# A decoder layer on one core: the down projection with moving weights and a seven-product block form

## The chip, the cores and the metric

The kernel runs on one core of a Trainium2 chip. The metric is device time in microseconds (us). The core's engines are TensorE (PE; PEld is its weight load), VectorE (DVE), ScalarE (ACT), GpSimd (POOL) and SyncE (SP, which only issues DMAs here; ACT issues some too). Each engine works through its own instructions in their written order.

## The reference

```python
o = concat(diff_attention(...), multiscale_pool(...)) ; x = x + o @ w_o
x = x + cross_attention(rmsnorm(x), rmsnorm(mem))              # ends with @ wo_x
hf = rmsnorm(x) * norm_ffn
x = x + (silu(hf @ w_gate) * (hf @ w_up)) @ w_down             # 2048 -> 5632 -> 2048
out = rmsnorm(x) * norm_final                                  # over the 2048 features
```

There are 256 tokens and 2048 features; all is float32. The change concerns the last two lines.

## The kernel before, in words

Every float32 product is made of float32r parts: a value is split into hi (a cast on ACT, L111) and lo = value - hi (a subtraction on DVE, L112), and a product is hi*hi + hi*lo + lo*hi, summed in PSUM. With a gain the split is L114 on ACT and L115 on DVE.

The residual stream x_sb and the activations lie transposed, features on partitions. In a projection to features (`gemm_feat`) the weight tile is stationary and 256 tokens move: for each k-tile of 128, one matmul of 512 columns (hi weights, both parts of the activations, L145) and one of 256 (lo weights, hi activations, L146). Weights come from HBM in loads of 1 MiB (L127, SP's queue, three buffers `raw`), and are split in halves `whi` and `wlo`, three buffers each, so that splits can run ahead of the matmuls. Where the result is wanted with tokens on partitions (`gemm_tok`, L191 to L193), the weights move in 512 columns, three matmuls a block.

The stages in order: input projection, attention and pooling, w_o (from 205 us), cross-attention (w_qx, w_kx, w_vx, w_ox), gate and up (w_gu, 672 us to 1177 us) and down (w_dn, to 1421 us). In the w_o stage the 256 memory tokens are also loaded (L505), split (L114, L115) and squared (L252 on ACT; L254 and L257 add on POOL), while x is updated (L262, L264), split again and its squares are summed (L268, L270 on POOL). Gate and up leave their tiles to DVE and ACT: L206 copies one part out of PSUM, L207 joins, L615 and L618 scale, L616 is Silu, L619 multiplies, and a split stores the activations.

Down is one more `gemm_feat`, with 16 feature tiles of 44 k-tiles; the last tile uses three matmuls of 256 columns (L199 to L201) to shorten its end. As each tile ends, x is updated, squared (L268) and multiplied by the final gain (L628); at the first tile a Sqrt is run early (L631). After the last tile: ones-matmuls add the squares over partitions (L236), Sqrt (L226), reciprocal (L227), a transpose spreads 1/rms along the free dimension (L246), and seven multiplications (L639) each feed an output DMA (L640).

A scheduler orders each engine's instructions; the order in the text is not the order that runs. `between` holds small pieces of work that it spreads among the weights.

Of the kernel before, what the change touches and what calls it, by code (L numbers as in the profile page):

```python
# [12 lines left out]
"""  # L13
# [18 lines left out]
P = 128  # L32
D = 2048
S = 256
# [8 lines left out]
FT = DFF // P  # L43
NB = D // 512

# columns of the array of per-partition parameters
# [5 lines left out]
def layer_kernel(ctx: ExitStack, tc: tile.TileContext, a: dict, out: bass.AP):  # L52
    nc = tc.nc
    const = ctx.enter_context(tc.tile_pool(name="const", bufs=1))
    act = ctx.enter_context(tc.tile_pool(name="act", bufs=15))
    wts = ctx.enter_context(tc.tile_pool(name="wts", bufs=3))
    tmp = ctx.enter_context(tc.tile_pool(name="tmp", bufs=5))
    row = ctx.enter_context(tc.tile_pool(name="row", bufs=4))
    st = ctx.enter_context(tc.tile_pool(name="st", bufs=4))
# [13 lines left out]
    def chunk():  # L73
        """4 k-tiles of split, transposed activations: [128, k-tile, hi / lo, 256 tokens]."""
        return slot().rearrange("p (j s t) -> p j s t", j=4, s=2)
# [45 lines left out]
    def weights(src, n=2048, piece=2048, load=None):  # L121
        """Up to 1 MiB of weights, as halves of (hi, lo)."""
# [50 lines left out]
    def gemm_tok(xT, src, load=None):  # L173
        """512 features of both token tiles: two of [128 tokens, 512]."""
# [22 lines left out]
    def mm3(ps, l, r, start=True, stop=True):  # L197
        """ps (+)= l.T @ r of split operands."""
# [4 lines left out]
    def joined(ps):  # L203
        """The sum of a feature tile's parts."""
# [5 lines left out]
    def features(xT, src, f0, n=4):  # L210
        """n feature tiles, split: a chunk."""
# [6 lines left out]
    def values(ps, r):  # L218
        """[128 tokens, hi / lo, token tile, 512 features] times the tokens' r."""
# [10 lines left out]
    def rms(*squares, rc=None):  # L230
        """1/rms of the tokens, with tokens on partitions: [128, 2]."""
# [10 lines left out]
    def along(rc):  # L242
        """The same along the free dimension, on every partition (in PSUM)."""
# [5 lines left out]
    def add_squares(tot, c, src):  # L249
        """The sum of squares of chunks of [128, 4 x 256], in the end as one tile."""  # L250
# [8 lines left out]
    def residual(f, ps, tot, g=None, into=None, one=False):  # L259
        """x += ps for a feature tile; its scaled split, and the squares added up."""  # L260
# [23 lines left out]
    # the tensor engine's clock rises while the first loads are under way  # L284
# [5 lines left out]
    hT = []  # L290

    def load_x(k):
        """k-tile k of x: the first eight one by one, then four at a time."""
# [5 lines left out]
        if j == 0:  # L299
            hT.append(chunk())  # L300
# [22 lines left out]
    # pooling: for every window the matrix of (window sum - count * token), and 1 / count  # L323
# [81 lines left out]
    def diff_head(h, qk):  # L405
# [29 lines left out]
        wps = misc().rearrange("p (k q) -> p k q", k=2)  # [128 keys, key tile, queries]  # L435
# [18 lines left out]
    def norm_heads(half, o):  # L454
        """Two heads' outputs: norm over 256 features, gain, transposed."""
# [69 lines left out]
    tot1 = t_row()  # L525
    hx = []
    for f, ps in gemm_feats(lambda: oT, a["w_o"]):
        if f % 4 == 0:
            hx.append(chunk())
        residual(f, ps, tot1, col(C_XAT + f), hx[-1])  # L530

# [16 lines left out]
    def cross_head(h, kx):  # L548
# [19 lines left out]
        pps = misc().rearrange("p (k q) -> p k q", k=2)  # [128 memory tokens, tile, queries]  # L568
# [28 lines left out]

    tot2 = t_row()
    hf = []
    for f, ps in gemm_feats(lambda: xo, a["w_ox"]):  # L600
        if f % 4 == 0:
            hf.append(chunk())
        residual(f, ps, tot2, col(C_FFN + f), hf[-1])

# [1 line left out]
    aT = []  # L606
    for f in range(FT):
        if f % 4 == 0:
            aT.append(chunk())
        ps = gemm_feat(hf, a["w_gu"][2 * f])  # L610
        if f == 0:
            rb_f = t_row()
            nc.vector.tensor_copy(out=rb_f, in_=along(rms(tot2)))
        g = joined(ps)
        nc.vector.tensor_tensor(out=g, in0=g, in1=rb_f, op=ALU.mult)  # L615
        nc.scalar.activation(out=g, in_=g, func=AF.Silu)  # L616
        y = joined(gemm_feat(hf, a["w_gu"][2 * f + 1]))
        nc.vector.tensor_tensor(out=y, in0=y, in1=rb_f, op=ALU.mult)  # L618
        nc.vector.tensor_tensor(out=g, in0=g, in1=y, op=ALU.mult)  # L619
        split(aT[-1][:, f % 4, 0], aT[-1][:, f % 4, 1], g)  # L620

# [1 line left out]
    tot3 = t_row()  # L623
    rc_y = const.tile([P, 2], F32, name="rc_y")
    for f in range(KT):
        last = f == KT - 1
        sq = residual(f, gemm_feat(aT, a["w_dn"][f], FT, one=last), tot3, one=last)
        nc.scalar.activation(out=x_sb[:, f], in_=x_sb[:, f], func=AF.Copy, scale=col(C_FIN + f))  # L628
        if f == 0:
            # the table of Sqrt is there before it is waited for  # L630
            nc.scalar.activation(out=rc_y, in_=tot3[:, :2], func=AF.Sqrt)  # L631
# [76 lines left out]
```

## Time and profile before

| | us |
|---|---|
| median of 3 runs | 1432.77 (1432.4 to 1434.15) |
| span of the profiled execution | 1431.9 |
| PE busy | 1417.8 (99%) |
| DVE busy | 897.3 (63%) |
| ACT busy | 715.0 (50%) |
| down stage, PE busy from 1176 to 1421 | 245.0 of 245 |
| from the last down matmul (1420.5) to the end | 11.4 |

The span is the time from the first to the last instruction of one profiled execution; the median is 0.87 us above it. A matmul's own duration is longer than its step: consecutive ones overlap, so the step is read from start to start. Idle time of DVE or ACT matters only where PE waits for it.

### The profile page before, as it was taken

How to read it: one execution, taken by the hardware profiler on the slowest of the kernel's cores; microseconds unless marked ns; L12 is line 12 of the kernel's file. 1: busy time of each engine (PE TensorE's matmuls, PEld its weight loads, DVE VectorE, ACT ScalarE, POOL GpSimd, SP SyncE). 2: the span in 40 equal slices, each digit the busy share in tenths (PEclk: the TensorE clock that was granted, in tenths of full speed). 3: DMA queues.
4: the chain of work that ended last, by engine and by line, in shares of the span. 5: the costliest groups of instructions: out<-in, count | busy, mean ns of one | idle time of the engine just before them, and what ended most of it. 6: DMA issues, size and time to landing. Idle time of an engine off the chain costs nothing.

```text
span 1431.9 us, 20153 instructions
## 1 busy us (share of the span) xinstructions
PE 1417.8 (99%) x8050; PEld 1240.2 (87%) x8050; DVE 897.3 (63%) x1229; ACT 715.0 (50%) x1064; POOL 104.6 (7%) x118
## 2 busy tenths in 40 slices
PE   8999999999999999999999999999999999999997
PEld 6888888888888888888888888888888888888886
DVE  6666867975556555577666666666666664454443
ACT  6555755664454444455544444444444444444442
POOL 3700001410000000011000000000000000010010
PEclk9999999999999999999999999999999999999999
DMA  7544436555544445365455555555555555555552
GB/s 267 205 169 171 173 121 246 182 204 184 199 176 164 163 167 180 122 219 192 177 195 187 189 193 182 201 181 202 178 200 182 195 181 191 184 191 194 182 194 107
DMA packets 41565, 264.54 MB, mean 185 GB/s; under 512 B 4736, under 2 KB 6016, under 8 KB 13312
## 3 DMA queue, kind: packets, MB, share of 16 engines
q1 hardware_dynamic: 41184, 262.69, 52.0%
q8 instruction: 63, 1.03, 0.3%
q10 hardware_dynamic: 288, 0.57, 0.1%
q14 instruction: 30, 0.25, 0.0%
HBM read 261.14 MB, written 2.10 MB: 184 GB/s over the span
## 4 chain that ended last, share of the span: by engine, by line
PE 97%; DVE 1%; DMA 1%; ACT 0%; SPq 0%; issue 0%; DVEq 0%; ACTq 0%
PE acc L145 53%; PE acc L146 28%; PE acc L192 4%; PE acc L193 4%; PE acc L191 4%; PE ms L200 1%; PE ms L201 1%; PE ms L199 1%; DMA raw<-in_w_vu 1%; DVE wlo L112 1%; PE acc L201 0%; PE acc L200 0%; PE acc L199 0%; DVE act L115 0%; PE ms L380 0%; DVE x_sb L639 0%
## 5 line engine op out<-in xcount | busy, mean ns | idle before, releaser
L145 PE MATMUL acc<-act,whi 128*128 128x512 f32 x3348 | 1169.6, 393 | 0.0
L146 PE MATMUL acc<-act,wlo 128*128 128x256 f32 x3348 | 938.4, 280 | 0.4 <-DVE wlo L112 0.3
L112 DVE TENSOR_TENSOR wlo<-raw,whi 128x1024 fp32r<-128x1024 f32 (+1 forms) x500 | 608.1, 1217 | 456.5 <-ACT whi L111 453.8
L111 ACT CAST whi<-raw 128x1024 fp32r<-128x1024 f32 (+1 forms) x500 | 515.1, 1030 | 583.0 <-PE acc L145 336.4
L145 PEld LDWEIGHTS acc<-act,whi 128*128 128x128 f32 x3348 | 627.0, 187 | 141.0
L146 PEld LDWEIGHTS acc<-act,wlo 128*128 128x128 f32 x3348 | 632.7, 189 | 1.5 <-DVE wlo L112 1.4
L270 POOL TENSOR_TENSOR row<-row,t 128x256 f32<-128x256 f32 x44 | 46.3, 1053 | 1151.4 <-ACT t L268 1151.4
L191 PE MATMUL acc<-whi,act 128*128 128x512 f32 x256 | 101.0, 396 | 1.8 <-ACT whi L111 1.8
L192 PE MATMUL acc<-wlo,act 128*128 128x512 f32 x256 | 100.7, 393 | 1.1 <-DVE wlo L112 1.0
L193 PE MATMUL acc<-whi,act 128*128 128x512 f32 x256 | 100.4, 392 | 0.0
L111 ACT CAST act<-t 128x256 fp32r<-128x256 f32 x92 | 37.1, 404 | 57.9 <-DVE t L207 57.4
L192 PEld LDWEIGHTS acc<-wlo,act 128*128 128x128 f32 x256 | 48.5, 190 | 12.4 <-DVE wlo L112 2.7
L191 PEld LDWEIGHTS acc<-whi,act 128*128 128x128 f32 x256 | 48.3, 189 | 12.3 <-ACT whi L111 2.7
L207 DVE TENSOR_TENSOR t<-acc,t 128x256 f32<-128x256 f32 x136 | 56.8, 418 | 1.3 <-ACT t L206 1.2
L193 PEld LDWEIGHTS acc<-whi,act 128*128 128x128 f32 x256 | 48.4, 189 | 10.2
L206 ACT COPY t<-acc 128x256 f32<-128x256 f32 x136 | 49.8, 366 | 0.4 <-PE acc L146 0.4
L112 DVE TENSOR_TENSOR act<-t,act 128x256 fp32r<-128x256 f32 x92 | 38.7, 421 | 17.6 <-ACT act L111 17.2
L115 DVE SCALAR_TENSOR_TENSOR act<-x_sb,sm,act 128x256 fp32r<-128x256 f32 x48 | 38.9, 821 | 0.4 <-ACT act L114 0.4
L262 DVE TENSOR_TENSOR x_sb<-acc,x_sb 128x256 f32<-128x256 f32 x48 | 20.1, 419 | 17.4 <-PE acc L146 11.4
L114 ACT ACTIVATE act<-x_sb,sm 128x256 fp32r<-128x256 f32 x48 | 23.8, 508 | 8.2 <-DVE x_sb L264 6.1
L268 ACT ACTIVATE t<-x_sb 128x256 f32<-128x256 f32 x45 | 18.3, 406 | 9.0 <-DVE x_sb L262 7.2
L264 DVE TENSOR_TENSOR x_sb<-acc,x_sb 128x256 f32<-128x256 f32 x47 | 19.8, 421 | 1.0
(144 smaller groups left out, 577.0 us busy)
## 6 DMA issues: line engine op xcount, KB each, us to landing
raw<-in_w_gu SPq DMA_DIRECT2D x88, 1024.0 KB, 4.8
raw<-in_w_dn SPq DMA_DIRECT2D x32, 1024.0 KB, 4.9
raw<-in_w_qk SPq DMA_DIRECT2D x16, 1024.0 KB, 4.8
raw<-in_w_qx SPq DMA_DIRECT2D x16, 1024.0 KB, 4.8
raw<-in_w_kx SPq DMA_DIRECT2D x16, 1024.0 KB, 4.8
raw<-in_w_vx SPq DMA_DIRECT2D x16, 1024.0 KB, 4.8
raw<-in_w_vu SPq DMA_DIRECT2D x12, 1024.0 KB, 4.8
raw<-in_w_o SPq DMA_DIRECT2D x12, 1024.0 KB, 4.8
```

Of the source, the lines that this page charges most:

```text
L111: nc.scalar.copy(out=hi, in_=src)
L112: nc.vector.tensor_tensor(out=lo, in0=src, in1=hi.bitcast(F32), op=ALU.subtract)
L114: nc.scalar.activation(out=hi, in_=src, func=AF.Copy, scale=g)
L115: nc.vector.scalar_tensor_tensor(out=lo, in0=src, scalar=g, in1=hi.bitcast(F32), op0=ALU.mult, op1=ALU.subtract)
L145: nc.tensor.matmul(ps, whi[:, w], x, start=(k == 0), stop=False)
L146: nc.tensor.matmul(ps[:, :S], wlo[:, w], x[:, 0], start=False, stop=(k == nk - 1))
L191: nc.tensor.matmul(ps[t], xh, whi[:, w], start=(k == 0), stop=False)
L192: nc.tensor.matmul(ps[t], xh, wlo[:, w], start=False, stop=False)
L193: nc.tensor.matmul(ps[t], xl, whi[:, w], start=False, stop=(k == KT - 1))
L206: nc.scalar.copy(out=y, in_=ps[:, S:])
L207: nc.vector.tensor_tensor(out=y, in0=ps[:, :S], in1=y, op=ALU.add)
L270: nc.gpsimd.tensor_tensor(out=tot, in0=tot, in1=sq, op=ALU.add)
```

## The change

The down projection is turned round. Activations are stationary (128 tokens of a k-tile), weights move in 512 columns, and the result has tokens on partitions. It runs in two halves of 1024 output columns (b) times 22 pairs of k-tiles (p). A pair is a 2 x 2 block product (2 token tiles x 2 k-tiles, times 2 k-tiles x 2 column blocks). For 15 pairs it is made of eight block products; for the seven pairs 0, 2, ..., 12 (FAST) of seven products of sums (a Strassen-Winograd form), the sums of the activations made in the gate and up stage (four DVE operations of 128 x 128 a pair), those of the weights in `prep` (L725, L727, L728), and the seven results recombined in `sums`. Each block product is three matmuls of 512 columns (`mm3`, L211 to L213).

The residual x must therefore be in rows: `to_rows` makes 32 PE transposes of 128 x 128 with 8 ACT copies, written to DRAM during w_ox and gate/up and read back later (L765). The final norm sums squares along the free dimension (ACT Square with its accumulator, L735), multiplies by a gain row (L736), and scales by 1/rms per partition (L843, L845); four output DMAs of 512 KB take the place of seven. Pools are rearranged: `act` has 11 buffers instead of 15, `hid` has 4 for the streamed activations, and the down stage's buffers (2 `raw`, 1 `sum`) lie on the memory of those that the gate and up stage has left.

```diff
+FAST = tuple(range(0, 14, 2))
-    act = ctx.enter_context(tc.tile_pool(name="act", bufs=15))
+    hid = up.enter_context(tc.tile_pool(name="hid", bufs=4, side="right"))
+    act = before.enter_context(tc.tile_pool(name="act", bufs=11))
...
+    def to_rows(q):
+        yield
+        for t in range(2):
+            yield
+            tp = misc()
+            for i in range(4):
+                nc.tensor.transpose(out=tp[:, i * P:(i + 1) * P], in_=x_sb[:, 4 * q + i, t * P:(t + 1) * P], identity=ident)
+            xr = t2()
+            nc.scalar.copy(out=xr, in_=tp)
+            nc.scalar.dma_start(out=x_dram[q // 2, :, t, (q % 2) * 512:(q % 2 + 1) * 512], in_=xr)
...
-    for f in range(KT):
-        last = f == KT - 1
-        sq = residual(f, gemm_feat(aT, a["w_dn"][f], FT, one=last), tot3, one=last)
...
+    def prep(b, p):
+        raw = dn_r.tile([P, 4, 512], F32, tag="raw", name=name("raw"))
+        nc.sync.dma_start(out=raw.rearrange("p s n -> p (s n)"), in_=a["w_dn"][b, p])
...
+        if p not in FAST:
+            yield halves(raw[:, 0:2], 2, dn_u, "u")
+            yield halves(raw[:, 2:4], 2, dn_u, "u")
+            return
+        s = dn_r.tile([P, 4, 512], F32, tag="sum", bufs=1, name=name("sum"))
+        nc.vector.tensor_tensor(out=s[:, 0:2], in0=b12[:, None].to_broadcast([P, 2, 512]), in1=raw[:, 0:2], op=ALU.subtract)
+        yield halves(raw[:, 0:3], 3, dn_a, "a")
+        nc.vector.tensor_tensor(out=s[:, 2], in0=b22, in1=s[:, 0], op=ALU.subtract)
+        nc.vector.tensor_tensor(out=s[:, 3], in0=b21, in1=s[:, 2], op=ALU.subtract)
+        yield halves(s[:, 0:2], 2, dn_u, "u")
+        yield halves(s[:, 2:4], 2, dn_u, "u")
...
+        for i, ps in enumerate(C):
+            y = ys[b][i // 2][:, (i % 2) * 512:(i % 2 + 1) * 512]
+            nc.vector.tensor_tensor(out=y, in0=ps, in1=y, op=ALU.add)
+            if b:
+                finished(b, i // 2, i % 2)
...
+            nc.vector.memset(ss, 1.0)
+            between.append(late())
+    for t in range(2):
+        r = const.tile([P, 1], F32, name=f"r{t}")
+        nc.vector.tensor_reduce(out=r, in_=ss[:, t], axis=AX.X, op=ALU.add)
+        rsqrt(r, r, D)
...
+            (nc.scalar if b == 0 else nc.sync).dma_start(out=out[:, t, b * 1024:(b + 1) * 1024], in_=y)
```

The first place is SP's queue in the w_o stage, before; the numbers behind the names are buffers, `raw` takes weights, `act` the memory tokens.

```order
L127 DMA raw_2294<-in_w_o 128x1024
L127 DMA raw_2324<-in_w_o 128x2048
L127 DMA raw_2375<-in_w_o 128x2048
L127 DMA raw_2425<-in_w_o 128x2048
L127 DMA raw_2479<-in_w_o 128x2048
L127 DMA raw_2532<-in_w_o 128x2048
L505 DMA act_2428<-in_memT 128x1024 x2
```

The same place in the changed kernel.

```order
L139 DMA raw_2302<-in_w_o 128x1024
L517 DMA act_2436<-in_memT 128x1024
L139 DMA raw_2332<-in_w_o 128x2048
L517 DMA act_2436<-in_memT 128x1024
L139 DMA raw_2383<-in_w_o 128x2048
L517 DMA act_2781<-in_memT 128x1024
L139 DMA raw_2433<-in_w_o 128x2048
L517 DMA act_2781<-in_memT 128x1024
```

The four loads of the memory tokens stand five and more weight loads earlier; their 16 splits on ACT (L126) and DVE (L127) and the POOL additions move with them.

The second place is ACT's queue in the changed kernel where gate and up end and down begins: `acc_10709` is the last up tile, `aC` a stored activation, `ah` and `uh` the hi parts of down's first weights.

```order
L654 COPY t1f_10752<-acc_10709 128x256
L123 CAST aC_10560<-t1f_10660 128x256
L765 DMA y_11120<-x_dram 128x1024 x2
L123 CAST ah_10787<-raw_10783 128x1536
L123 CAST uh_10802<-sum_10785 128x1024
L123 CAST uh_10812<-sum_10785 128x1024
```

DVE's queue at the same place, in the changed kernel.

```order
L655 TENSOR_TENSOR t1f_10752<-acc_10709,t1f_10752 128x256
L688 TENSOR_TENSOR t1f_10752<-t1f_10752,rb_f 128x256
L690 TENSOR_TENSOR t1f_10660<-t1f_10704,t1f_10752 128x256
L124 TENSOR_TENSOR aC_10560<-t1f_10660,aC_10560 128x256
L725 TENSOR_TENSOR sum_10785<-raw_10783 128x1024
L727 TENSOR_TENSOR sum_10785<-raw_10783,sum_10785 128x512
L728 TENSOR_TENSOR sum_10785<-raw_10783,sum_10785 128x512
L124 TENSOR_TENSOR al_10788<-raw_10783,ah_10787 128x1536
L124 TENSOR_TENSOR ul_10803<-sum_10785,uh_10802 128x1024
```

All work on down's first weights stands behind the finishing of the last up tile, on both engines; before, the first split of down (L111, L112) stood ahead of it.

The third place is the end: DVE in the changed kernel, `acc` the four results of the second half, `g` the gain row.

```order
L822 TENSOR_TENSOR y_11931<-acc_11587,y_11931 128x512
L822 TENSOR_TENSOR y_11932<-acc_11588,y_11932 128x512
L736 TENSOR_TENSOR y_11931<-y_11931,g_11973 128x512 x2
L736 TENSOR_TENSOR y_11932<-y_11932,g_11973 128x512
L822 TENSOR_TENSOR y_11932<-acc_11589,y_11932 128x512
L838 TENSOR_REDUCE r_12426<-ss 128x1
```

ACT there, in the changed kernel.

```order
L735 ACTIVATE d_12423,ss<-y_11932 128x512
L238 ACT_TABLE_LOAD
L238 ACTIVATE r_12426<-r_12426,eps 128x1
L238 ACTIVATE r_12434<-r_12434,eps 128x1
L843 ACTIVATE y_11120<-y_11120,r_12426 128x1024
```

Three gain multiplications stand ahead of the last addition, and a table load between the last Square and Sqrt. The early Sqrt that the text has in `late` (L830), with its table load, stands at ACT's very start, ahead of the first split of x.

## Rows read from the trace of the kernel before

**Rows 1.** The page: span; chain of waits, share of the span by engine

```profile
span 1431.9 us, 20153 instructions
...
PE 97%; DVE 1%; DMA 1%; ACT 0%; SPq 0%; issue 0%; DVEq 0%; ACTq 0%
```

**Rows 2.** Windows: length, busy us of PE, PEld, DVE, ACT, POOL; clock; DMA share; GB/s

```profile
672.00:1176.00 504.00, 504.00 (x2910) 444.14 (x2909) 327.94 (x455) 246.28 (x366) 3.80 (x4) 1.00 0.53 189
1176.00:1421.00 245.00, 245.00 (x1458) 217.94 (x1456) 116.98 (x129) 106.57 (x128) 18.95 (x14) 1.00 0.53 177
```

**Rows 3.** Timeline of PE: start, duration, line; pairs, last tile, moving weights

```profile
1178.74 0.39 PE L145 MATMUL acc<-act,whi 128*128 128x512 f32 x1
...
1180.47 0.39 PE L145 MATMUL acc<-act,whi 128*128 128x512 f32 x1
...
1413.75 0.28 PE L199 MATMUL acc<-act,whi 128*128 128x256 f32 x1
...
1420.47 0.28 PE L201 MATMUL acc<-act,wlo 128*128 128x256 f32 x1
...
59.66 0.39 PE L191 MATMUL acc<-whi,act 128*128 128x512 f32 x1
...
62.38 0.39 PE L191 MATMUL acc<-whi,act 128*128 128x512 f32 x1
```

**Rows 4.** Timeline of ACT where down begins

```profile
1177.32 0.37 ACT L206 COPY t<-acc 128x256 f32<-128x256 f32 x1
```

**Rows 5.** Timeline of DVE where down begins

```profile
1177.45 1.23 DVE L112 TENSOR_TENSOR wlo<-raw,whi 128x1024 fp32r<-128x1024 f32 x1 [1.81 <-ACT whi L111]
1178.59 0.42 DVE L207 TENSOR_TENSOR t<-acc,t 128x256 f32<-128x256 f32 x1
```

**Rows 6.** The page: cast of weights; busy us, mean ns

```profile
L111 ACT CAST whi<-raw 128x1024 fp32r<-128x1024 f32 (+1 forms) x500 | 515.1, 1030 | 583.0 <-PE acc L145 336.4
```

**Rows 7.** Groups of DVE in the down stage: count, busy us, mean ns

```profile
L112 DVE TENSOR_TENSOR wlo<-raw,whi 128x1024 fp32r<-128x1024 f32 x78 | 95.4, 1223 | 104.9 <-ACT whi L111 104.9
L112 DVE TENSOR_TENSOR wlo<-raw,whi 128x512 fp32r<-128x512 f32 x16 | 11.1, 692 | 17.4 <-ACT whi L111 17.4
```

**Rows 8.** Timeline of PE in the start, idle before in brackets

```profile
20.06 0.73 PE L191 MATMUL acc<-whi,act 128*128 128x512 f32 x2 [1.14 <-ACT whi L111]
...
22.93 0.63 PE L192 MATMUL acc<-wlo,act 128*128 128x512 f32 x1
23.36 0.63 PE L193 MATMUL acc<-whi,act 128*128 128x512 f32 x1
```

**Rows 9.** Windows in the w_o stage

```profile
228.00:256.00 28.00, 28.00 (x162) 24.29 (x161) 24.59 (x35) 17.80 (x29) 5.04 (x6) 1.00 0.69 250
266.00:286.00 20.00, 19.57 (x108) 16.29 (x107) 19.48 (x20) 12.98 (x20) 14.51 (x8) 1.00 0.52 199
```

**Rows 10.** Timeline of DVE in the w_o stage: two memory splits; a weight split

```profile
267.45 0.89 DVE L115 SCALAR_TENSOR_TENSOR act<-act,sm,act 128x256 fp32r<-128x256 f32 x2
...
279.40 2.65 DVE L112 TENSOR_TENSOR wlo<-raw,whi 128x1024 fp32r<-128x1024 f32 x1
```

**Rows 11.** Timeline of POOL in the w_o stage

```profile
278.45 2.52 POOL L254 TENSOR_TENSOR act<-act 128x1024 f32<-128x1024 f32 x1 [1.17 <-ACT act L252]
```

**Rows 12.** Timeline of PE: eight transposes, from first start to last end

```profile
159.17 1.03 PE L469 MATMUL ms<-ident,act 128*128 128x128 f32 x8
```

**Rows 13.** Timeline of SP's queue: the first six of seven output DMAs

```profile
1424.15 3.62 SPq L640 DMA_DIRECT2D out<-x_sb  x6
```

**Rows 14.** Timeline of ACT: a table load and what follows

```profile
45.63 1.28 ACT L226 ACT_TABLE_LOAD   x1
46.93 0.26 ACT L226 ACTIVATE rc<-ms,eps 128x1 f32<-128x1 f32 x1
```

**Rows 15.** DMA issues: KB, median us to landing; down's weights

```profile
raw<-in_w_dn SPq DMA_DIRECT2D x32, 1024.0 KB, 4.9
```

**Rows 16.** DMA issues from 235 to 300

```profile
act<-in_memT SPq DMA_DIRECT2D x4, 512.0 KB, 6.4
```

More of the change, by code (lines that the diff above doesn't have):

```diff
@@ L601, in layer_kernel @@
         if f % 4 == 0:
-            hf.append(chunk())
+            hf.append(chunk(True))
         residual(f, ps, tot2, col(C_FFN + f), hf[-1])
[L606 to L620, printed above, removed]
@@ L635, in layer_kernel @@
[L635 to L641 removed]
+        if f % 4 == 3:
+            between.append(to_rows(f // 4))
+    ps_g = gemm_feat(hf, a["w_gu"][0])
+    rb_f = const.tile([P, S], F32, name="rb_f")
@@ new lines, in layer_kernel, with t1f, joined_f @@
+    nc.vector.tensor_copy(out=rb_f, in_=along(rms(tot2)))
+    ps_u = gemm_feat(hf, a["w_gu"][1])
+    finish()
+    before.close()
+    aTp = ctx.enter_context(tc.tile_pool(name="aT", bufs=1, reuse_waits="tile"))
+    t1p = up.enter_context(tc.tile_pool(name="t1p", bufs=6, reuse_waits="tile"))
+    A11, A12, A22, S1, S2, S3, S4, A21 = range(8)
+    sides = []
+    def t1f():
+        return t1p.tile([P, S], F32, tag="t1f", name=name("t1f"))
+    def joined_f(ps):
+        y = t1f()
+        nc.scalar.copy(out=y, in_=ps[:, S:])
+        nc.vector.tensor_tensor(out=y, in0=ps[:, :S], in1=y, op=ALU.add)
+        return y
@@ new lines, in finished, with sums @@
+    def finished(b, t, h):
+        y = ys[b][t][:, h * 512:(h + 1) * 512]
+        nc.scalar.activation(out=d512(), in_=y, func=AF.Square, accum_out=ss[:, t, 2 * b + h:2 * b + h + 1])
+        nc.vector.tensor_tensor(out=y, in0=y, in1=gs[b][:, h * 512:(h + 1) * 512], op=ALU.mult)
+    def sums(b, M):
+        y = [[ys[b][t][:, h * 512:(h + 1) * 512] for h in range(2)] for t in range(2)]
+        add = lambda o, x, z: nc.vector.tensor_tensor(out=o, in0=x, in1=z, op=ALU.add)
+        p1, u2, u3 = d512(), d512(), d512()
+        nc.scalar.copy(out=p1, in_=M[0])
+        yield
+        add(u2, M[3], p1)
+        yield
+        add(u3, M[4], u2)
+        add(y[0][0], y[0][0], p1)
+        yield
+        add(y[1][0], y[1][0], u3)
+        add(u2, M[2], u2)
+        yield
+        add(y[0][1], y[0][1], u2)
+        add(u3, M[2], u3)
+        yield
+        add(y[1][1], y[1][1], u3)
@@ new lines, in load_rows, with load_gains @@
+    def load_rows(b):
+        if b == 0:
+            t = dec.tile([P, 2, 1024], F32, tag="y", bufs=1, name="y0")
+            ys[b] = [t[:, 0], t[:, 1]]
+        else:
+            ys[b] = [aTp.tile([P, 1024], F32, tag="C", bufs=FP - len(FAST), name=name("y1")) for _ in range(2)]
+        for t in range(2):
+            nc.scalar.dma_start(out=ys[b][t], in_=x_dram[b, :, t])
+        yield
+    def load_gains():
+        for b in range(2):
+            gs[b] = aTp.tile([P, 1024], F32, tag="C", bufs=FP - len(FAST), name=name("g"))
+            nc.scalar.dma_start(out=gs[b], in_=a["gain"][:, b * 1024:(b + 1) * 1024].to_broadcast([P, 1024]))
+        yield
@@ new lines, in layer_kernel, with into, late @@
+    pending = []
+    for b in range(2):
+        M = {}
+        C = [acc() for _ in range(4)]
+        def into(ps, w, n, p, last=False):
+            mm3(ps, sides[p][n], w, id(ps) not in M, last or (p in FAST[-1:] and any(ps is q for q in shared)))
+            M[id(ps)] = True
+        shared = [misc() for _ in range(4)] if FAST else []
+        for p in range(FP):
+            parts = prep(b, p)
+            if p in FAST:
+                b11, b22, b21 = next(parts)
+                tick()
+                into(shared[0], b11, A11, p)
+                into(C[1], b22, S4, p)
+                into(C[0], b21, A12, p)
+                s1, s3 = next(parts)
+                into(shared[1], s1, S1, p)
+                into(shared[3], s3, S3, p)
+                tick()
+                s2, s4 = next(parts)
+                into(shared[2], s2, S2, p)
+                into(C[2], s4, A22, p)
+            else:
+                b11, b22 = next(parts)
+                tick()
+                into(C[0], b11, A11, p)
+                into(C[2], b11, A21, p)
+                into(C[1], b22, A12, p)
+                into(C[3], b22, A22, p)
+                b21, b12 = next(parts)
+                tick()
+                last = p == FP - 1
+                into(C[0], b21, A12, p, last)
+                into(C[1], b12, A11, p, last)
+                into(C[2], b21, A22, p, last)
+                into(C[3], b12, A21, p, last)
+            if p == 8 or (not FAST and p == 0):
+                between.append(load_rows(b))
+            if b == 1 and p == 9:
+                between.append(load_gains())
+            if p == 14 and FAST:
+                between.append(sums(b, [shared[0], None, shared[1], shared[2], shared[3]]))
+        finish()
+        for i, ps in enumerate(C):
[3 more added lines that the diff above has]
+                finished(b, i // 2, i % 2)
+        if b == 0:
+            def late():
+                for _ in range(26):
+                    yield
+                nc.scalar.activation(out=ss[:, :, 0], in_=ss[:, :, 0], func=AF.Sqrt)
+                for i in range(4):
+                    finished(0, i // 2, i % 2)
+                    yield
+            nc.vector.memset(ss, 1.0)
+            between.append(late())
```

109 lines of the change are left out of this document (81 added, 28 removed).

## Prediction

> **What bounds the kernel now.** I read the chain of waits first: 97% of it is PE [rows 1]. The windows by stage say the same of the two stages that matter most here: gate and up, and down, have PE busy in every microsecond, while DVE is busy 117 of 245 us in down [rows 2]. So a matmul taken away from down is time saved, one for one, and anything that makes PE wait, or gives it other work, is time added. The timeline of PE then gives the steps. Five pairs of a 512- and a 256-column matmul take 1180.47 - 1178.74 = 1.73 us, 0.346 each; the last tile takes 6.72 us for 56 steps, 0.120 each; where weights move, twelve 512-column matmuls take 2.72 us, 0.2267 each [rows 3]. Last I read the three places at which the order changes: the w_o stage, the seam between gate/up and down, and the end.
>
> **The matmuls.** Before: 15 x 44 pairs x 0.346 = 228.4, and 132 x 0.120 = 15.8, together 244.2 us, which agrees with the window of 245. After: 2 halves x (15 pairs x 8 + 7 pairs x 7) products x 3 = 1014 matmuls x 0.2267 = 229.9 us. This is **-14.3 us**. The moving-weight rows are float32r matmuls of the same shape, each with a new stationary tile, so I carry nothing for the form.
>
> The Trainium skill, "TensorE: Matmul & The Clock Gate", section "Back-to-back issue gap", gives N / 2.4 + 2.5 ns for an isolated matmul at full clock, which is 215.7 ns at 512 columns. The rows show 226.7, so the trace does not agree. By the page the 1014 matmuls would be 11.2 us shorter; it comes back as a rival.
>
> **The seam, +6.3.** In the order after, ACT and DVE do nothing for down's first weights until the last up tile is finished. From the end of its last matmul, when ACT's copy starts [rows 4]: the copy 0.37, three DVE operations of 0.42 with some 0.03 between [rows 5], so 1.7; the cast of the stored activation about 0.4; two DMA issues in ACT's queue, for which no row stands alone, at most 3.62 / 6 = 0.6 each [rows 13], taken as 0.3 each; then the cast of 1536 columns, one and a half times 1.03 [rows 6], 1.55. With hand-overs that is 4.5 us before PE has a first hi part. The weights themselves landed earlier. The lo part comes later: DVE ends the activation's split at 2.6, then L725 1.22, L727 and L728 0.69 each, and a split of 1536 columns, 1.83 [rows 7], is ready at 7.0. PE can run only four hi matmuls (0.9 us) in the meantime, so it loses 7.0 - 0.9 = 6.1, and a little more as the next lo parts come, 1.2 us each against six matmuls of 1.36. I take 6.3, with bounds 4.5 (lo parts cost nothing) and 8 (DMA issues at 0.6 and slower hand-overs). Before, DVE's first split of down's weights started 1177.45, ahead of the join of the last tile [rows 5], and PE lost nothing.
>
> **The clock, +0.8.** In the start PE stood for 1.14 us and its step was then 0.43 us, twice the usual, in 22.93 to 23.36 [rows 8], the level of 1.2 GHz instead of 2.4. The seam's idle time is longer. If as many as eight matmuls then cost 0.2 more, it is 1.6, but half of that falls where PE waits for lo parts anyway. Bounds 0 and 2.
>
> **Rows of x, +3.4.** Eight transposes took 1.03 us from the first start to the last end, the last overlapping what follows; about 0.107 each [rows 12]. 32 of them are PE work that was not there: 3.4 us (up to 4.1 by 1.03 / 8). The 8 ACT copies, the DMAs to and from DRAM and the four 128-column sums of each FAST pair lie in stages where DVE is busy 328 of 504 us and ACT 246 [rows 2]: nothing, and at most 2 us if one of them delays a split.
>
> **The w_o stage, +3.8.** The memory tokens' splits and additions now fall into the part where x is updated and split. There DVE is busy 24.59 of 28 us with four of the sixteen memory splits in it [rows 9]. The other twelve bring 12 x 0.45 = 5.3 us [rows 10], and three POOL additions of 2.5 us [rows 11] come too: beside one, a split of 1.22 took 2.65 [rows 10], 1.4 more each, 4.3 in all. That is 9.6 against 3.4 of spare time, 6.2 too many. The buffers let splits lead: three halves of 8 pairs x 0.346 = 2.8 us each, less the one that is read, 5.5 us at most. I let 2.4 of that be there. Bounds 0 and 6.2. The four memory DMAs stand ahead of weight loads in SP's queue, but three buffers of weights cover half a MiB each.
>
> **The start, +0.7.** The early Sqrt and its table load stand ahead of the first split of x; ACT waits there for data until shortly after the load would be done. Squares of x, about 1 us each, stand among the first splits, and PE waits for ACT there already [rows 8]. Bounds -1 and +2.
>
> **The end, +2.7.** Before, the first output DMA was issued 3.68 us after the last matmul's start (1420.47 to 1424.15) and the end came 7.75 us behind that [rows 1, 3, 13]. After, counted from the last matmul's start: three gain multiplications (0.69 each) begin at about 0.1, the last addition ends at 2.9, Square with its accumulator 0.8, table load 1.28, Sqrt 0.26 [rows 14], the reciprocal about 0.2, the scaling of 1024 columns 0.7 to 1.05, and hand-overs: 6.4. The 2 MB after it are the same. Bounds +0.5 (four large DMAs drain faster) and +4.
>
> The Trainium skill, "ScalarE: Activation LUTs", section "What ACT_TABLE_LOAD costs", adds a drain of about 1.38 us to each load of 1.283. Here the activation starts at 46.93, right behind the load of 45.63 [rows 14], so the trace does not show the drain as a gap; by the page the end would be 1.4 us later still.
>
> **The seven-product pairs, 0.** A FAST pair and the plain one behind it have 45 matmuls, 10.2 us. DVE does L725 1.22, L727 and L728 1.38, splits of 1.83, 1.22 and 1.22, and 2 x 1.22 for the plain pair, 9.3 us [rows 7]: hidden, by 9%. A raw buffer is held 1.22 + 0.69 + 1.83 + 0.69 = 4.4 us and then needs a landing of 4.9 [rows 15]: 9.3 as well. If the cover goes, see the first rival.
>
> **Sum:** -14.3 + 6.3 + 0.8 + 3.4 + 3.8 + 0.7 + 2.7 = +3.4 us on the span of 1431.9, 1435.3; the median of the runs stood 0.87 above that span, so I forecast **1436.2 us**. A change of this kernel of less than about 0.2%, 2.9 us, can't be told from none.
>
> **Rivals.**
>
> *The FAST part becomes the bound.* Place: the two raw buffers in pairs 0 to 13 of each half. 512 KB of memory tokens took 6.4 us to land among other loads [rows 16]. With 6.4 the buffer's round is 10.9 instead of 9.3, 0.7 over PE's 10.2, fourteen times: +10, 1446. It decides from a landing of about 5.8. For it: a margin of 9% on both. Against: down's loads landed in 4.9, and the rate rises only from 177 GB/s [rows 2] to some 205.
>
> *The w_o stage absorbs its work: not slower.* Place: DVE from 232 to 260. If the splits lead by the full 5.5 us and the POOL additions meet fewer DVE operations, the 3.8 vanish, and the sum is -0.4: 1432.4. It decides from a lead of about 5 us. For it: before, 266 to 286 had DVE busy 19.48 of 20 us with PE losing 0.43 [rows 9]. Against: the lead was gone there, and now more work comes in the same time.
>
> *Matmuls step as columns alone would have it.* With 0.2157 instead of 0.2267 us the down matmuls take 218.7, and the whole 1425. Against: every moving-weight row of this kernel. The page named above is the reason to keep it at all.
>
> *The form doesn't save what it says.* If the recombination in `sums` (ten operations of 512 columns on DVE, twice) held PE, some 3 us more: 1439. It runs among plain pairs, where DVE needs 2.44 of 5.4 us.
>
> **How the numbers follow.** Forecast 0.53, its own range 1433 to 1440: 0.35 of it above the bound of 0.2%, 0.16 within, 0.02 below. FAST part as bound 0.17, slower. w_o absorbed 0.20: 0.13 within, 0.07 faster. Short steps 0.04, faster. Sums that hold PE, and what I have not seen, 0.06: 0.03 slower, 0.02 faster, 0.01 within. Together faster 0.15, no change 0.30, slower 0.55. The range is 1430 to 1447: below it lie the short steps and some of the absorbed case, above it the worst of the FAST case.
>
> **What would show it.** Down's first moving matmul starts 4 to 5 us after the last up matmul, and the second in the same PSUM tile 2 us later; the clock's row is lower there. Down's 512-column steps are 0.227 and PE is without gaps in the FAST part; gaps at every second pair, released by a DMA or a lo split, would be the first rival. PE gaps of 3 to 4 us in sum stand between 235 and 262, released by lo splits of w_o. The first output DMA is issued more than 6 us behind the last matmul. If the seam loses under 3 us, or the end is no later than before, the forecast is wrong on its largest terms.

## The result, and the profile after

The changed kernel takes 1448.9 us (median of 4 runs, 1447.67 to 1450.29) against 1433.46 (4 runs, 1432.4 to 1434.72) for the kernel before: a ratio of 1.011, 95% interval 1.0096 to 1.0125. The forecast was 1436.2, within 1430 to 1447. The direction was right, the size was not: the runs grew by 15.4 us and the profiled span by 16.7, not by 3.4. The profiled run, 1450.29, is the longest of the four.

The page of the changed kernel, span and chain, answers [rows 1]; the share of DVE went from 1 to 4%.

```profile
span 1448.6 us, 19291 instructions
...
PE 93%; DVE 4%; DMA 1%; ACT 1%; issue 1%; SPq 0%; DVEq 0%; ACTq 0%
```

The windows of gate and up, and of down (columns as in [rows 2]):

```profile
702.00:1191.00 489.00, 489.00 (x2827) 427.52 (x2825) 322.89 (x460) 239.95 (x349) 0.95 (x1) 1.00 0.54 188
1196.00:1434.00 238.00, 237.28 (x1010) 191.72 (x1009) 175.10 (x168) 112.90 (x112) 0.00 (x0) 0.99 0.56 197
```

PE has no idle time of note inside either. I laid the two traces side by side by the first and last matmul of each stage. This is where the span's +16.7 came in:

| stretch | predicted us | measured us |
|---|---|---|
| start, to the first matmul of w_qk | +0.7 | +5.2 |
| w_o stage (97.2 to 102.5) | +3.8 | +5.3 |
| w_vx (99.1 to 101.2) | 0 | +2.0 |
| w_ox and gate/up (transposes in them) | +3.4 | +2.9 |
| seam: last up matmul to first down matmul | +4.5 (hi parts) | +4.7 |
| down, first to last matmul (244.5 to 239.2) | -11.7 (matmuls -14.3, lo parts +1.8, clock +0.8) | -5.3 |
| last matmul to the end (11.4 to 13.7) | +2.7 | +2.3 |

The other stages make -0.5. PE's waits in the changed kernel (us in total, times, longest):

```profile
PE acc L204 <- DVE wlo L124: 6.5, 5, 3.4
PE ms L211 <- ACT ah L123: 4.5, 1, 4.5
PE acc L158 <- DVE wlo L124: 3.6, 2, 2.5
PE acc L203 <- ACT whi L123: 1.1, 2, 0.6
...
PE ms L212 <- DVE al L124: 0.7, 1, 0.7
```

L204 and L203 are the start, L158 is w_o, L211 and L212 are the seam. They explain most of what the start, w_o and the seam lost. They say nothing of down and w_vx: there PE was busy all the time and yet slower. That shows in PE's timeline, in the step from start to start. Two 512-column matmuls of down, twelve steps apart:

```profile
1299.63 0.39 PE L213 MATMUL acc<-uh,aC 128*128 128x512 f32 x1
...
1302.42 0.39 PE L213 MATMUL acc<-uh,aC 128*128 128x512 f32 x1
```

That is 2.79 / 12 = 0.2325 us each (0.2324 over the stage), where the moving weights before took 0.2267 [rows 3]. Over 1014 matmuls the difference is 5.8 us. The same step appears in w_vx, where before it was 0.2273 over the stage. The durations (0.39) are the same at either step, and a busy share of 100% hides the difference.

**The start.** POOL, DVE and PE of the changed kernel, in that order:

```profile
21.50 2.74 POOL L266 TENSOR_TENSOR act<-act 128x1024 f32<-128x1024 f32 x1 [2.79 <-ACT act L264]
25.94 2.44 POOL L266 TENSOR_TENSOR act<-act 128x1024 f32<-128x1024 f32 x1 [1.70 <-ACT act L264]
...
22.39 2.93 DVE L124 TENSOR_TENSOR wlo<-raw,whi 128x1024 fp32r<-128x1024 f32 x1 [0.41 <-ACT whi L123]
25.25 4.83 DVE L127 SCALAR_TENSOR_TENSOR hid<-x_sb,sm,hid 128x256 fp32r<-128x256 f32 x4
30.00 5.09 DVE L124 TENSOR_TENSOR wlo<-raw,whi 128x1024 fp32r<-128x1024 f32 x3
...
31.79 0.50 PE L204 MATMUL acc<-wlo,hid 128*128 128x512 f32 x1 [3.39 <-DVE wlo L124]
```

A split of 1.22 us took 2.93 beside a POOL addition, and four splits of x of 1.7 us took 4.83. In the kernel before, POOL's first addition of squares of x stands here:

```profile
27.40 2.48 POOL L254 TENSOR_TENSOR act<-act 128x1024 f32<-128x1024 f32 x1 [20.91 <-ACT act L252]
```

In the changed kernel the first stands at 16.33: the squares need an `act` buffer, and since the activations have a pool of their own (`hid`), nothing holds that buffer back. (That the pool held them back is read from the order; no run has this change alone.) They now fall among the first weight splits, where no split is ready ahead. How much the start loses differs: in the four traces whose start is that of the changed kernel, w_qk begins 2.9 to 5.2 us later than before (83.3 here, 80.9 in e1_pad, 82.7 in e3_memory, 82.0 in e4_eight).

**The w_o stage.** The additions for the memory tokens do the same among the splits there (POOL, DVE, PE):

```profile
240.96 2.92 POOL L266 TENSOR_TENSOR act<-act 128x1024 f32<-128x1024 f32 x1 [1.09 <-ACT act L264]
...
241.54 2.62 DVE L127 SCALAR_TENSOR_TENSOR hid<-x_sb,sm,hid 128x256 fp32r<-128x256 f32 x1
...
254.13 0.39 PE L158 MATMUL acc<-act,wlo 128*128 128x256 f32 x1 [1.05 <-DVE wlo L124]
...
262.95 0.38 PE L158 MATMUL acc<-act,wlo 128*128 128x256 f32 x1 [2.55 <-DVE wlo L124]
```

Three such meetings (at 241, 249 and 257) cost a DVE operation of 0.5 some 2.1 us each. PE waited 3.6 us longer in the stage than before (3.9 against 0.3), of the 5.3 that it lost. Most of the rest stands behind the longer wait, in this window (third number from the end: the granted clock):

```profile
263.90:268.00 4.10, 4.10 (x17) 3.53 (x16) 3.87 (x6) 2.28 (x4) 0.73 (x1) 0.58 0.45 150
```

Behind the 2.55 idle us PE ran here at a granted clock of 0.58, and six pairs took 3.6 us instead of 2.1.

**The seam.** ACT, DVE and PE:

```profile
1191.15 0.37 ACT L654 COPY t1f<-acc 128x256 f32<-128x256 f32 x1 [3.80 <-PE acc L158]
1192.93 0.40 ACT L123 CAST aC<-t1f 128x256 fp32r<-128x256 f32 x1 [1.41 <-DVE t1f L690]
1192.93 0.81 ACTq L765 DMA_DIRECT2D y<-x_dram  x2
1194.12 1.47 ACT L123 CAST ah<-raw 128x1536 fp32r<-128x1536 f32 x1 [0.79 <-ACT aC L123]
...
1196.29 1.75 DVE L124 TENSOR_TENSOR al<-raw,ah 128x1536 fp32r<-128x1536 f32 x1
...
1195.64 0.50 PE L211 MATMUL ms<-ah,aS 128*128 128x512 f32 x1 [4.54 <-ACT ah L123]
1198.10 0.80 PE L212 MATMUL ms<-al,aS 128*128 128x512 f32 x1 [0.72 <-DVE al L124]
```

And the window behind it (the granted clock is again the third number from the end):

```profile
1195.60:1202.90 7.30, 6.54 (x15) 4.59 (x16) 6.95 (x7) 3.80 (x5) 0.00 (x0) 0.53 0.64 240
```

The order is the one predicted: join, cast of the activation, DMA issues, cast of `ah`. After 4.5 idle us PE runs at a granted clock of 0.53, about the lower level (1.2 GHz), for 7 us, and a step is 0.43. By then the lo parts of `al` are wanted, so much of the wait that I expected for them is hidden behind slow matmuls: 0.72 is left. Wait and slow steps together make down's first matmuls 3.8 us longer than their number times 0.2324.

**The end.** DVE, ACT and SP's queue:

```profile
1435.22 1.89 DVE L736 TENSOR_TENSOR y<-y,g 128x512 f32<-128x512 f32 x3
...
1438.54 1.28 ACT L238 ACT_TABLE_LOAD   x1
1439.84 0.48 ACT L238 ACTIVATE r<-r,eps 128x1 f32<-128x1 f32 x2
...
1441.14 1.20 SPq L846 DMA_DIRECT2D out<-y  x2
```

The first output DMA is issued 6.26 us behind the last matmul's start (1434.88), against 3.68 before [rows 3, 13].

### The profile page after: what moved, and what is told of

It is laid out like the page before. It is cut to its first block, busy times and chain, and to the rows that moved or that the text cites. A ratio compares the mean times of both kernels' runs of the same rounds, so it can differ in the third digit from the quotient of the medians.

```text
span 1448.6 us, 19291 instructions
## 1 busy us (share of the span) xinstructions
PE 1417.2 (98%) x7634; PEld 1215.7 (84%) x7634; DVE 968.7 (67%) x1298; ACT 732.0 (51%) x1058; POOL 83.0 (6%) x103
## 4 chain that ended last, share of the span: by engine, by line
PE 93%; DVE 4%; DMA 1%; ACT 1%; issue 1%; SPq 0%; DVEq 0%; ACTq 0%
PE acc L157 41%; PE acc L158 21%; PE acc L213 5%; PE acc L212 4%; PE acc L211 4%; PE acc L205 4%; PE acc L203 4%; PE acc L204 4%; PE ms L212 2%; PE ms L213 2%; PE ms L211 2%; DVE wlo L124 1%; DVE act L127 1%; DVE hid L127 1%; DMA x_sb<-in_xT 1%
## 5 line engine op out<-in xcount | busy, mean ns | idle before, releaser
L124 DVE TENSOR_TENSOR wlo<-raw,whi 128x1024 fp32r<-128x1024 f32 (+1 forms) x404 | 495.7, 1228 | 332.6 <-ACT whi L123 329.9
L157 PE MATMUL acc<-hid,whi 128*128 128x512 f32 x1920 | 669.2, 395 | 0.0
L158 PE MATMUL acc<-hid,wlo 128*128 128x256 f32 x1920 | 533.1, 278 | 0.0
L157 PEld LDWEIGHTS acc<-hid,whi 128*128 128x128 f32 x1920 | 360.3, 188 | 83.5
L158 PEld LDWEIGHTS acc<-hid,wlo 128*128 128x128 f32 x1920 | 360.9, 188 | 0.0
L157 PE MATMUL acc<-act,whi 128*128 128x512 f32 x768 | 273.1, 396 | 0.3 <-DVE act L127 0.3
L158 PE MATMUL acc<-act,wlo 128*128 128x256 f32 x768 | 218.0, 284 | 3.7 <-DVE wlo L124 3.6
L157 PEld LDWEIGHTS acc<-act,whi 128*128 128x128 f32 x768 | 145.0, 189 | 33.1 <-DVE act L127 0.6
L158 PEld LDWEIGHTS acc<-act,wlo 128*128 128x128 f32 x768 | 145.4, 189 | 4.8 <-DVE wlo L124 4.7
L213 PE MATMUL acc<-uh,aC 128*128 128x512 f32 x240 | 94.7, 395 | 0.0
L211 PE MATMUL acc<-uh,aC 128*128 128x512 f32 x240 | 94.7, 395 | 0.0
L212 PE MATMUL acc<-ul,aC 128*128 128x512 f32 x240 | 94.7, 395 | 0.0
L204 PE MATMUL acc<-wlo,hid 128*128 128x512 f32 x128 | 51.1, 399 | 6.6 <-DVE wlo L124 6.5
L212 PEld LDWEIGHTS acc<-ul,aC 128*128 128x128 f32 x240 | 45.2, 189 | 10.6
L213 PEld LDWEIGHTS acc<-uh,aC 128*128 128x128 f32 x240 | 45.2, 188 | 10.6
L211 PEld LDWEIGHTS acc<-uh,aC 128*128 128x128 f32 x240 | 45.2, 189 | 10.4
L203 PE MATMUL acc<-whi,hid 128*128 128x512 f32 x128 | 50.8, 401 | 1.1 <-ACT whi L123 1.1
```

Source lines behind the costliest of these rows:

```text
L157: nc.tensor.matmul(ps, whi[:, w], x, start=(k == 0), stop=False)
L158: nc.tensor.matmul(ps[:, :S], wlo[:, w], x[:, 0], start=False, stop=(k == nk - 1))
L203: nc.tensor.matmul(ps[t], xh, whi[:, w], start=(k == 0), stop=False)
L204: nc.tensor.matmul(ps[t], xh, wlo[:, w], start=False, stop=False)
L211: nc.tensor.matmul(ps, l[0], r[0], start=start, stop=False)
L212: nc.tensor.matmul(ps, l[0], r[1], start=False, stop=False)
```

## The experiments

Theory: the slower step comes from where the operands lie. By the addresses in the built programs, `act` and the weights both begin at 32 modulo 256 bytes before; in the changed kernel `act` and the stored activations begin at 96, the weights at 224, 128 apart. Gate and up, whose activations (`hid`) begin at 224 as well, kept their step. The rival is the form: new stationary tiles out of sums, other PSUM tiles, more DMA. The start and w_o are to be tested by putting the POOL additions back where they were. The first four kernels ran together (before: 1432.46, 7 runs). The changed kernel did not run beside them; the kernel before took 1.0 us less there than beside it, so the gains below, counted from 1448.9, can be up to 1 us too large.

**e1_pad**: one constant tile of 128 bytes more, so that every operand pool begins at 224 modulo 256.

```diff
+    pad = const.tile([P, 32], F32, name="pad")
+    nc.gpsimd.memset(pad, 0.0)
     ones = const.tile([P, P], F32, name="ones")
```

> The changed kernel with one unused tile of 128 bytes a partition ahead of the other tiles on the left side of SBUF, and a memset of it on POOL; nothing else. Activations (act, aC, aS) then start at the same address modulo 256 as the weights on the right side (224; before the edit 96 against 224). Placement theory: the down step falls from 0.2324 to 0.2267 us and the w_vx step from 0.2327 to 0.2277; 997 x 0.0057 + 256 x 0.005 = 7 us less, and the pairs of w_o, w_kx and w_ox move from 0.351; about 1441. Rival (the seven-product form, or a state of PE that the idle time at the seam leaves): steps stay at 0.2324, time within 1 us of 1449.

Measured: 1439.54 (1439.15 to 1441.49), 9.4 below the changed kernel. A window of down of the changed kernel, then of e1_pad (length, PE busy and instructions, clock, DMA share, GB/s):

```profile
1210.00:1410.00 200.00, 200.00 (x862) 1.00 0.59 208
```

```profile
1210.00:1410.00 200.00, 200.00 (x884) 1.00 0.61 215
```

With PE busy throughout in both, 862 matmuls against 884: from start to start 0.2324 and 0.2267 us each. Down took 232.3 us instead of 239.2, and w_vx's step fell back to 0.227 too. The placement theory stands. Down (6.9) and w_vx (2.0) make 8.9 us. Of the 6.9, 5.8 are the step; 1.2 are fewer slow matmuls at the seam, which no edit touched and which vary between traces. The span fell by 10.6, since this trace's start was 2.3 shorter as well, the medians by 9.4.

**e2_squares**: the squares of x are taken in the opposite order, so that the first needs the part of x that comes last.

```diff
-            add_squares(tot, c, x_sb[:, 4 * c:4 * c + 4].rearrange("p j t -> p (j t)"))
+            add_squares(tot, c, x_sb[:, 12 - 4 * c:16 - 4 * c].rearrange("p j t -> p (j t)"))
```

> The changed kernel with x's squares taken from the last four k-tiles first, so that the first Square waits for the last load of x; ACT then has the four squares after the splits of x, as before the change. Theory (the early squares and their POOL additions slow the first splits): PE's waits in the first 60 us fall from 8.8 us to about 4, w_qk starts 4 to 5 us earlier, 1444. Rival (the early Sqrt and its table load, or other loads, delay the start): no change, 1449; the table load stands where it was.

Measured: 1444.44 (1443.71 to 1446.69), 4.5 below. POOL's first addition now stands at 25.57. PE's waits in e2_squares at the start:

```profile
PE acc L204 <- DVE wlo L124: 1.8, 4, 0.5
PE acc L203 <- ACT whi L123: 1.4, 2, 1.2
```

7.6 us of waiting are 3.2, and in this trace w_qk begins 5.1 us earlier than in the changed kernel's.

**e3_memory**: the memory tokens are loaded later. A copy of one column of x makes each load wait for a tile of w_o.

```diff
-        for _ in range(12):
+        for _ in range(20):
             yield
...
+                    nc.vector.tensor_copy(out=raws[:, i * 1024:i * 1024 + 1], in_=x_sb[:, 3 + c + i, :1])
```

> The changed kernel with the memory tokens' loads held back until x's feature tiles 3 to 6 have been updated in the w_o stage (a one-column copy of x into the buffer ahead of the load, overwritten by it). Theory (the memory tokens' splits and additions crowd DVE among the first updates of x): the w_o stage falls from 102.5 to about 98 us, 1445. Rival (the stage is longer for another reason, as the place of the activations): 102, 1449.

Measured: 1444.04 (1443.46 to 1444.17), 4.9 below. PE's wait in w_o, in e3_memory:

```profile
PE acc L158 <- DVE wlo L124: 0.8, 2, 0.5
```

POOL's three additions beside the updates of x at 241, 249 and 257 are gone from there (one is left, at 258.62). In this trace the stage takes 97.3 us, about what it took before the change (97.2), instead of 102.5.

**e4_eight**: all 22 pairs by eight products.

```diff
-FAST = tuple(range(0, 14, 2))
+FAST = ()
```

> The changed kernel with all 22 pairs made of eight products: 1056 matmuls in down instead of 1014. If the seven-product pairs save what their count says: 42 x 0.2324 = 9.8 us more in down, less about 1.5 for the first pair's lo parts, which come sooner; 1457. Rival (the sums of the seven-product pairs cost as much as they save): 1449 or less. Placement theory: the step stays 0.2324 here too; the rival that the form causes it: 0.2267, and 1451.

Measured: 1458.26 (1457.54 to 1460.91), 9.4 above. A window of down in e4_eight:

```profile
1210.00:1410.00 200.00, 200.00 (x860) 1.00 0.59 206
```

The step is that of the changed kernel without any seven-product pair, so the form isn't its cause. The form saves 14 products of three matmuls, 42 x 0.2324 = 9.8 us. Without it down grew by 8.8 and the seam by 1.6, and the whole by 9.4: about what the form promises, so what DVE does for it is hidden.

**e5_before_shifted** (this and the next three ran together; before: 1432.84, 20 runs): the kernel before with a pool of 128 bytes between the activations and the weights.

```diff
     act = ctx.enter_context(tc.tile_pool(name="act", bufs=15))
+    gap = ctx.enter_context(tc.tile_pool(name="gap", bufs=1))
+    g0 = gap.tile([P, 32], F32, name="g0")
+    nc.gpsimd.memset(g0, 0.0)
```

> The kernel before with an unused tile of 128 bytes a partition between the activations and the weights, so that the two lie 128 apart modulo 256 (32 and 160), and a memset of it on POOL. Placement theory, worked out on the steps seen in the changed kernel (0.351 a pair where the two lie apart, 0.3467 or 0.353 where not; 0.2325 against 0.2270 with moving weights): gate/up and down 1364 pairs x 0.0042 = 5.7 us more, the pairs of w_qx and w_kx that ran at 0.3467 some 1 us more, w_vu and w_vx 760 matmuls x 0.005 = 3.8 more, those that ran at 0.353 about 1.5 less: +9, 1441.5. Rival (the place matters only in the changed kernel's arrangement): 1432.5.

Measured: 1444.44 (1444.18 to 1444.65), +11.6: 128 bytes that nothing reads make the kernel before 0.8% slower. Windows of gate/up and down, of the kernel before and then of e5_before_shifted:

```profile
720.00:1170.00 450.00, 450.00 (x2598) 1.00 0.53 190
1210.00:1410.00 200.00, 200.00 (x1169) 1.00 0.56 186
```

```profile
720.00:1170.00 450.00, 450.00 (x2565) 1.00 0.52 188
1210.00:1410.00 200.00, 200.00 (x1141) 1.00 0.55 188
```

The pairs slow down too, from 0.3467 to 0.3511. Over some 2070 pairs of gate/up and down that alone is about 9 us, where the expectation counted 1364 pairs; w_vx adds 2.0. In the start the slower step lengthened nothing, and w_ox, which ran at 0.3533 a pair before, became 0.5 us shorter.

**e6_three**: the edits of e1_pad, e2_squares and e3_memory together.

> The changed kernel with the three edits of e1 (128 bytes), e2 (x's squares last first) and e3 (memory tokens held back) together. If the three causes are apart, their effects add: 1448.9 - 9.4 - 4.5 - 4.9 = 1430.1, 0.2% under the kernel before. Rival (they share a cause, such as DVE being behind for long): 1434 or more.

Measured: 1431.5 to 1432.71 in four runs and 1439.54 to 1442.54 in eight, nothing between. Counted from the kernel before of each set of runs, the changed kernel is 15.4 us longer and the three gains are 8.4, 3.5 and 3.9, so their sum puts this kernel 0.2 below the kernel before; the lower group is 0.1 to 1.3 below. The upper, two thirds of the runs, I had not foreseen.

**e7_plain_first**: e6_three with the seven-product pairs at 1, 3, ..., 13, so that down begins with a plain pair.

```diff
-FAST = tuple(range(0, 14, 2))
+FAST = tuple(range(1, 15, 2))
```

> As e6, with pairs 1, 3, ..., 13 made of seven products instead of 0, 2, ..., 12, so that down begins with a plain pair. Theory of the seam (the chain of the last up tile, then the sums L725, L727, L728 and the long splits ahead of the first lo part): the idle time up to the first matmul falls by 0.4 us (a cast of 1024 instead of 1536) and that up to the first lo part from 7 to about 5.5: 1.5 less than e6, less a little for the clock. Rival (the clock's recovery and the first landing set it): within 0.5 of e6.

Measured: again two groups, 1430.61 to 1432.2 (three runs) and 1438.24 to 1444.3 (six). PE waited 4.7 us at the seam, against 4.3 plus 0.7 in e6_three: no gain that can be told. But its profiled run was one of the upper group (1440.56), and that of e6_three one of the lower (1431.74). The window of gate/up of e6_three, then of e7_plain_first:

```profile
720.00:1170.00 450.00, 450.00 (x2598) 1.00 0.53 186
```

```profile
720.00:1170.00 450.00, 450.00 (x2549) 1.00 0.53 187
```

The whole stage runs at 0.353 a pair instead of 0.3467, with no gap and the clock at 1.00 in both: 1382 pairs x 0.0066 = 9.1 us, the distance of the groups. That is a comparison of two kernels: no kernel was traced in both groups. The step is settled at the stage's start; PE's work other than pairs there, in e7_plain_first:

```profile
694.73 0.50 PE L248 MATMUL ms<-ones,row 128*128 128x1 f32 x4
697.95 0.38 PE L258 MATMUL ms<-ident,rc 128*128 128x128 f32 x2
698.17 1.04 PE L623 MATMUL ms<-ident,x_sb 128*128 128x128 f32 x8
```

Behind L248 the pairs step at 0.347 in both traces; behind the eight transposes at 698.17 they stay at 0.3467 in e6_three and go to 0.3533 in e7_plain_first. The kernel before has no such transposes. But they alone don't make a second group. They stand at the same place, last, in the changed kernel and in e1_pad to e4_eight, and there each kernel's four runs, 20 in all, lie within 3.4 us, and all five traces have 0.3467; e1_pad's transposes and window:

```profile
706.58 1.04 PE L622 MATMUL ms<-ident,x_sb 128*128 128x128 f32 x8
```

```profile
720.00:1170.00 450.00, 450.00 (x2598) 1.00 0.55 190
```

**e8_gain_last**: e6_three with the gain of the second half multiplied in with 1/rms.

```diff
-        nc.vector.tensor_tensor(out=y, in0=y, in1=gs[b][:, h * 512:(h + 1) * 512], op=ALU.mult)
+        if b == 0:
+            nc.vector.tensor_tensor(out=y, in0=y, in1=gs[b][:, h * 512:(h + 1) * 512], op=ALU.mult)
...
-                nc.vector.tensor_scalar(out=y, in0=y, scalar1=r, scalar2=None, op0=ALU.mult)
+                nc.vector.scalar_tensor_tensor(out=y, in0=y, scalar=r, in1=gs[b], op0=ALU.mult, op1=ALU.mult)
```

> As e6, without the four gain multiplications of the second half ahead of the sums; the gain goes into the last scaling on DVE (y x 1/rms x gain in one operation of 1024 columns, 1.2 instead of 0.76 us). Theory of the end (three gain multiplications, 1.9 us, stand between the third addition and the last): the last Square starts 1.9 us sooner, the first output DMA 1.4 sooner: e6 - 1.5. Rival (the 2 MB of output set the end, whenever they start): e6 - 0 to 0.5.

Measured: 1439.81 (1434.96 to 1441.64), the profiled run at 0.353 a pair. The two steps cover what the edit does: inconclusive, taken up in e10. One run, 1434.96, lies in neither group, and no trace says why.

**e9_rows_early** (with e10; before: 1433.34, 21 runs): e6_three with one line, which issues the transposes of the last quarter of x ahead of the norm's work.

```diff
     ps_g = gemm_feat(hf, a["w_gu"][0])
+    finish()
     rb_f = const.tile([P, S], F32, name="rb_f")
```

> e6_three with one line more: the transposes of the last quarter of the residual stream are issued ahead of the ones-products of the norm, instead of behind its transposes, so that the last work of TensorE other than pairs ahead of the 1382 pairs of the gate and up stage is the pair of transposes of the norm, as in the kernel before. In e6_three the stage ran at a step of 0.3467 a pair (run of 1431.7), in e7_plain_first and e8_gain_last at 0.3533 (runs of about 1440), each time from the pairs right behind those transposes of the residual stream. Theory (the step of the stage is settled by what stood last on TensorE): every run between 1430 and 1433, step 0.3467. Rival (the two steps are drawn anew in any order of the work): runs at 1431 to 1433 and at 1439 to 1443 again, some 9 us apart.

Measured: 1431.78, all 11 runs in 1429.57 to 1434.45, no second group. PE's other work at the stage's start, in e9_rows_early:

```profile
693.30 0.82 PE L623 MATMUL ms<-ident,x_sb 128*128 128x128 f32 x6
693.95 0.51 PE L248 MATMUL ms<-ones,row 128*128 128x1 f32 x4
...
698.88 0.38 PE L258 MATMUL ms<-ident,rc 128*128 128x128 f32 x2
```

And its window of gate/up:

```profile
720.00:1170.00 450.00, 450.00 (x2599) 1.00 0.52 186
```

Ahead of the row of pairs the norm's transposes now stand last, as in the kernel before, and no run shows a second group, here or in e10. That this order removed it is likely, not shown: e6_three, e7_plain_first and e8_gain_last ran on one chip, e9 and e10 on another, and e1_pad to e4_eight, with the old order and one group, on a third. A run of e6_three beside e9 would have told the order from the chip.

**e10_rows_early_gain_last**: e9_rows_early with the edit of e8_gain_last.

> e9_rows_early with the gain multiplied in with the last factor of each row tile, as in e8_gain_last, which takes the multiplication of 1.9 us out of the end. Theory: 1.5 to 2 us below e9_rows_early, thus 1428.5 to 1431, 2 to 4 us under the kernel before. Rival: the end is bound by the second half's sums and its square, and the time is that of e9_rows_early.

Measured: 1430.57 (11 runs, 1429.76 to 1431.45), 1.2 below e9_rows_early and 2.8 below the kernel before: ratio 0.9982, interval 0.9973 to 0.9991. DVE, ACT and SP's queue at its end, where the last matmul started at 1416.70:

```profile
1415.09 2.73 DVE L827 TENSOR_TENSOR y<-acc,y 128x512 f32<-128x512 f32 x4 [6.53 <-PE acc L213]
...
1418.65 1.28 ACT L238 ACT_TABLE_LOAD   x1
...
1421.79 1.74 SPq L851 DMA_DIRECT2D out<-y  x2
```

The last addition ends at 1.1 us behind the last matmul's start instead of 2.8, the table load starts at 1.95 instead of 3.66. Part is given back, as the longer L850 (1.28 us instead of 0.76) stands behind 1/rms. This version beats both kernels, the kernel before by little: 2.8 us is about what the prediction took for the least that can be told from none, and it is told here by 11 runs against 21.

## Why the prediction was wrong in size

By its own steps:

- **The matmuls: mis-sized, and the largest miss.** "I carry nothing for the form": the form indeed cost nothing (e4_eight), but the rearranged pools moved the operands, and the step of 0.2267 was carried over to operands that lie otherwise. 1014 x 0.2324 = 235.7, so the term was -8.5 instead of -14.3, and w_vx, which the change doesn't touch in the text, lost 2.0. e1_pad gave both back with one unused tile. Without the shift the term was right: down took 232.3 us in e1_pad, of which 2.7 are the slow first matmuls and lo waits of the seam. The rival of shorter steps (0.2157, by the rule for an isolated matmul in the Trainium skill's "TensorE: Matmul & The Clock Gate", section "Back-to-back issue gap") did not come in any run: the shortest step is 0.2267.
- **The start: wrong mechanism.** I weighed the early Sqrt and ACT's queue and gave +0.7, bounds -1 and +2. It was +5.2 in this trace and at least +2.9 in three others, from POOL's additions, which came 11 us earlier and slowed DVE's splits. I saw the squares move in ACT's order, and did not follow them on to POOL, although I had the price of such a meeting for w_o [rows 10, 11]. e2_squares brought 4.5 of it back.
- **The w_o stage: right mechanism for the wait, the clock behind it left out.** +5.3 against +3.8, inside its bounds of 0 and 6.2. PE waited 3.6 us longer, about the 3.8 forecast; in part by luck, since a meeting with POOL cost 2.1 us and not 1.4, and the lead of the splits was then more than the 2.4 I let them. The 1.5 us at the lower clock behind the longer wait I had priced at the seam only. e3_memory brought 4.9 back.
- **Seam and clock: right mechanism, 1.4 too small, inside the bounds.** 7.1 predicted; 4.7 idle and 3.8 over in down make 8.5 (7.4 in e1_pad). The split between them was off: the clock took some 3.1 instead of 0.8 and the lo parts 0.7 instead of 1.8, since the slow matmuls gave them time.
- **Rows of x and the end: right** in their first sizes, 2.9 for 3.4 (3.4 in e1_pad, where w_ox has its old step) and 2.3 for 2.7. At the end Sqrt starts right behind its table load (1438.54 + 1.28), as in [rows 14]. What I missed of the transposes came out only in e7_plain_first: behind them the step of 1382 pairs can be another.
- **Seven-product pairs: right.** PE has no gap there, and e4_eight shows 9.4 of the 9.8 us arriving. The first rival did not come.

By the rows of the table the misses are 6.4 in down (5.8 of it the step), 4.5 in the start, 2.0 in w_vx, 1.5 in w_o and 0.2 at the seam, 14.6 together, less 1.4 on rows, end and the other stages: 13.2 of the 13.3 us between the forecast of the span and the span. What is left of the sum holds: without the terms of w_o and the start it is -1.1, and e6_three's lower group and e9_rows_early, which have the three misses undone, lie 0.1 to 1.6 below the kernel before.

Open: what in the positions makes the step, since only offsets of 0 and 128 bytes were tried; and what leads to one step or the other behind the eight transposes, since e6_three took both with one order and the kernels before it took one. A trace shows that little is enough: in e10_rows_early_gain_last the pairs of w_o go from 0.3533 to 0.3467 behind a single step that was 0.03 us late (260.41 to 260.68), with no other work of PE between.

## What to carry to other kernels

When a change moves pools, compare the addresses of the matmul's two operands before and after, also for stages that the change doesn't touch, and read steps from start to start: PE's busy share shows nothing of it. When a pool is split, ask which work its buffers had held back, and follow that work onto every engine it reaches. Where PE is forecast to wait, price the slow matmuls behind the wait too. If runs of one kernel fall into two groups, compare a trace of each by the count of instructions in a window before averaging them, and run the kernel that has the groups beside the one that is to be without.

## What the runs showed of the hardware that was not expected

- Matmuls whose stationary and moving operands begin 128 bytes apart modulo 256 step at 0.2324 us for 512 columns (0.2333 in e2_squares) instead of 0.2267, and a pair of 512 and 256 columns at 0.351 instead of 0.3467, at a granted clock of 1.00 (e1_pad, e5_before_shifted).
- Pairs with aligned operands have two steps, 0.3467 and 0.3533, one below and one above the 0.351 of pairs that lie apart, and keep one for 1382 pairs on end (e6_three, e7_plain_first). The step changed behind other work of PE (e9_rows_early) and once behind a step that was 0.03 us late (e10_rows_early_gain_last).
